# One layer of a hybrid decoder trunk on one core: reciprocal roots of the head norms moved from GpSimd to ScalarE and VectorE, a later and denser pace of head work, six part tiles in the down product, and a last block finished by halves

## The chip, the cores and the metric

The kernel runs on one core of one Trainium2 chip. The metric is the device time of one execution in microseconds (us), as the median of several runs. The engines are called by the names of the profile: PE is TensorE (matmuls), PEld its weight loads, DVE is VectorE, ACT is ScalarE, POOL is GpSimd, and SP is SyncE, whose queue issues nearly all of the kernel's DMA transfers, in the order of the program.

## The reference

One layer, 512 tokens, model width 2048, everything in float32:

```python
h = rms_norm(x, g)
p = h @ w_in                   # split: GLA q, k (512 each), v, r (1024 each), gate 16, attention q, k, v (1024 each)
A = gla_mixer(...)             # 4 heads, dk 128, dv 256; o = rms_norm(o) * silu(r) at its end
B = dilated_mixer(...)         # 8 heads of 128; q and k are normalised per head; three dilation patterns
x = x + concat(A, B) @ w_out
x = x + (silu(n @ w_gate) * (n @ w_up)) @ w_down     # n = rms_norm(x, g2), hidden width 5632
```

Two kinds of small norm matter here. Each head's q and k rows are divided by the root of their mean square over 128 columns, and each GLA output row by that over its 256 columns. The factor is (mean + eps)^(-1/2), one number per row and head.

## The kernel before

**The large products.** Every large product is done by one level of a scheme with seven products (in the order P1, P5, P6, P3, P7, P2, P4) in place of eight. The program names a piece of work a *pair*: two blocks of 512 output columns by 512 rows. There is one first pair with an order of its own, and 18 streamed ones: five for w_in (the last of them computes the gate r, "the gate pair"), two for w_out, eleven for the gate and up products of the feed-forward part, and six for w_down, which is the product "down": three thirds of the 5632 rows (i = 0, 1, 2) by two column halves (`np_` = 0, 1). A streamed pair has 28 items (21 in the last third of down). An item is one 128x1024 weight tile against an operand that is already in SBUF.

**One item.** float32 values are split in a high and a low part. For an item ACT casts the weight tile to the high part `wh` (L371), DVE subtracts to get the low part `wl` (L375), and PE does twelve 128x512 matmuls: eight with `wh`, four with `wl` (L398). `wh` and `wl` have two buffers each. Where an item's weight is a sum of two blocks, DVE forms that first (L296). The accumulators `acc` are two banks per product, for the two halves m = 0, 1 of its 256 rows; in every item the matmuls alternate between m = 0 and m = 1. When a product is done, DVE and ACT add its banks into `seed` tiles (L322, L334, L338), and `final` hands finished 128x512 blocks on.

**Work between the items.** After the eighth matmul of an item `p.step()` lets generators in the background do some units of their own: the eight attention heads, the GLA heads, the splitting of operands. How many units go into each item is set by a pace: for the gate pair `scripted(rate((27, 0.72), (1, 0)), GATE)` at L1219, which means 0.72 of a unit per item for 27 items, counted up, so that units fall on items 1, 2, 4, 5, 6, 8, 9, 11, 12, 13, 15 and so on. `hold=True` makes the sums of the pair wait behind the heads' instructions. Heads 4 to 7 become ready at the end of the pair ahead (columns 3584 and 4608, the q and k of these heads): its last blocks, called `cout`, are normalised by `heads_norm` and stored to a DRAM buffer `qb`, and the first unit of the heads (`dil_head`) loads from there the tiles q, qT, k and kT (L924 to L928), which PE transposes with an identity from `mats` (L935), ACT copies (L936), and from which PE makes scores (L944), DVE and ACT the softmax (L947 to L954), PE transposes again (L961) and multiplies with the values (L968). All instructions of an engine run in the order of the program; the heads' stand between those of the items.

**The norms' factor.** `rsqrt_mean` (L179 to L181) is called 24 times: 16 times in `heads_norm` on a tile `ss` of 128x4, and 8 times at L890 on a tile `so` of 128x2. It is two POOL instructions: multiply and add, then a power of -0.5 by a tensor `mhalf`. Ahead of it ACT has done Squares with sums (L1019 into `ss`, L889 into `so`); behind it DVE multiplies (L1021, L892) and SP stores (L1046).

**Operands of down.** The left operands of a third of down are fetched from DRAM in parts of 128x512 by `fetch_part` (L1148, DMA at L1152) into four tiles with the tags v, T, qT, kT in turn. ACT casts a part to the high half (L196), DVE subtracts the low half (L197) into the operand tiles `AA` and `AS`. `staged(items, 2)` (L1404) keeps the loads two parts ahead of the splitting. The parts of thirds 1 and 2 come during the second column half of the third ahead.

**Residual and end.** `final_down` (L1421) calls `residual` (L1229), which loads the earlier sum from `x1_d` or `y_d` into the tiles q and k (L1235) and adds it with DVE (L1237 where the accumulator is added in directly, L1240 where a `seed` tile is); the result is stored to `y_d` (L1433) or `out` (L1431). The last block of all is that of P4 in the last pair: two 128x512 halves that are added (L1237) and stored (L1431) when the last matmul is done.

## Time and profile before

| | |
|---|---|
| median of 3 runs | 1948.6 us (1947.58 to 1950.29) |
| profiled execution | 1952.11 us |
| its span, first to last instruction | 1950.0 us |
| mean granted TensorE clock | 0.998 |
| PE busy | 1916.9 us (98%), 9160 matmuls |
| DVE busy | 1647.6 us (84%) |
| ACT busy | 1088.9 us (56%) |
| POOL busy | 47.2 us (2%), 73 instructions |

The span begins with the first instruction and ends with the last one, so that 2.1 us of the profiled execution's time lie outside of it. A row of the timeline gives start, duration, engine, line, operation, output and inputs, and in square brackets how long the engine had been idle ahead of it and whose result ended that. A row of the windows gives a stretch of time, its length, the busy time of PE, PEld, DVE, ACT and POOL with the number of instructions, then the granted clock of PE, the share of the DMA engines and GB/s. SPq is the moment at which SP issues a transfer; the chain of waits has the time that the transfer itself takes.

### The profile page before, as it was taken

How to read it: one execution, taken by the hardware profiler on the slowest of the kernel's cores; microseconds unless marked ns; L12 is line 12 of the kernel's file. 1: busy time of each engine (PE TensorE's matmuls, PEld its weight loads, DVE VectorE, ACT ScalarE, POOL GpSimd, SP SyncE). 2: the span in 40 equal slices, each digit the busy share in tenths (PEclk: the TensorE clock that was granted, in tenths of full speed). 3: DMA queues.
4: the chain of work that ended last, by engine and by line, in shares of the span. 5: the costliest groups of instructions: out<-in, count | busy, mean ns of one | idle time of the engine just before them, and what ended most of it. 6: DMA issues, size and time to landing. Idle time of an engine off the chain costs nothing.

```text
span 1950.0 us, 25512 instructions
## 1 busy us (share of the span) xinstructions
PE 1916.9 (98%) x9160; PEld 1660.6 (85%) x9160; DVE 1647.6 (84%) x1845; ACT 1088.9 (56%) x1580; POOL 47.2 (2%) x73
## 2 busy tenths in 40 slices
PE   7999999999999999999999999999999999999998
PEld 6788888887888888888888888888888888888887
DVE  7996877767799999878878878878879989989987
ACT  8654564566676675544544544544546646546443
POOL 0000230001000000000000000000000000000000
PEclk9999999999999999999999999999999999999999
DMA  9445555454535563454464454453555765855662
GB/s 354 170 151 205 171 189 154 149 164 150 176 138 186 184 224 117 138 178 162 135 189 148 144 184 137 155 184 121 171 172 180 270 217 177 292 195 180 235 216 76
DMA packets 150791, 347.84 MB, mean 178 GB/s; under 512 B 15542, under 2 KB 42463, under 8 KB 150664
## 3 DMA queue, kind: packets, MB, share of 16 engines
q1 hardware_dynamic: 150520, 346.21, 53.5%
q8 instruction: 71, 1.16, 0.2%
q14 instruction: 56, 0.46, 0.1%
q10 hardware_dynamic: 144, 0.01, 0.0%
HBM read 288.20 MB, written 60.31 MB: 179 GB/s over the span
## 4 chain that ended last, share of the span: by engine, by line
PE 72%; DVE 7%; DMA 3%; issue 2%; ACT 1%; SPq 0%; POOLq 0%; POOL 0%; DVEq 0%; ACTq 0%
PE acc L398 68%; DVE wl L375 3%; PE bank L1059 1%; DVE wa L296 1%; PE bank L944 1%; PE bank L968 1%; DVE AS L197 1%; DMA wc<-in_w_in 0%; DMA p_d<-PT 0%; PE bank L935 0%; PE bank L961 0%; ACT wh L371 0%; DMA r<-p_d 0%; ACT jk L1019 0%; DMA q<-in_x 0%
## 5 line engine op out<-in xcount | busy, mean ns | idle before, releaser
L398 PE MATMUL acc<-wh,AS 128*128 128x512 f32 x3008 | 711.1, 379 | 0.0
L398 PEld LDWEIGHTS acc<-wh,AS 128*128 128x128 f32 x3008 | 568.6, 189 | 81.1 <-ACT wh L371 0.4
L371 ACT CAST wh<-wa 128x1024 fp32r<-128x1024 f32 x376 | 394.2, 1049 | 397.8 <-PE acc L398 357.7
L398 PE MATMUL acc<-wh,AA 128*128 128x512 f32 x2256 | 533.7, 379 | 2.8 <-ACT wh L371 2.8
L375 DVE TENSOR_TENSOR wl<-wa,wh 128x1024 fp32r<-128x1024 f32 x376 | 457.2, 1218 | 68.0 <-ACT wh L371 42.2
L398 PEld LDWEIGHTS acc<-wh,AA 128*128 128x128 f32 x2256 | 426.0, 189 | 64.5 <-ACT wh L371 4.0
L398 PE MATMUL acc<-wl,AS 128*128 128x512 f32 x1504 | 396.3, 385 | 3.9 <-DVE wl L375 3.8
L398 PEld LDWEIGHTS acc<-wl,AS 128*128 128x128 f32 x1504 | 280.1, 189 | 55.4 <-DVE wl L375 13.6
L398 PE MATMUL acc<-wl,AA 128*128 128x512 f32 x1128 | 295.1, 384 | 0.0
L398 PEld LDWEIGHTS acc<-wl,AA 128*128 128x128 f32 x1128 | 210.0, 189 | 29.8 <-issue 1.0
L371 ACT CAST wh<-wb 128x1024 fp32r<-128x1024 f32 x94 | 98.5, 1048 | 124.0 <-PE acc L398 118.4
L371 ACT CAST wh<-wc 128x1024 fp32r<-128x1024 f32 x94 | 98.5, 1047 | 110.8 <-PE acc L398 106.5
L371 ACT CAST wh<-wd 128x1024 fp32r<-128x1024 f32 x94 | 98.6, 1049 | 101.9 <-PE acc L398 93.3
L375 DVE TENSOR_TENSOR wl<-wc,wh 128x1024 fp32r<-128x1024 f32 x94 | 114.6, 1220 | 41.0 <-ACT wh L371 41.0
L375 DVE TENSOR_TENSOR wl<-wd,wh 128x1024 fp32r<-128x1024 f32 x94 | 114.4, 1219 | 38.9 <-ACT wh L371 30.1
L296 DVE TENSOR_TENSOR wa<-wc,wa 128x1024 f32<-128x1024 f32 x94 | 114.4, 1220 | 34.0 <-DMA wc<-in_w_gate 20.6
L375 DVE TENSOR_TENSOR wl<-wb,wh 128x1024 fp32r<-128x1024 f32 x94 | 114.1, 1217 | 4.8 <-ACT wh L371 4.5
L296 DVE TENSOR_TENSOR wa<-wb,wa 128x1024 f32<-128x1024 f32 x94 | 113.6, 1219 | 1.1 <-DMA wb<-in_w_in 0.4
L296 DVE TENSOR_TENSOR wb<-wd,wb 128x1024 f32<-128x1024 f32 x94 | 114.1, 1217 | 0.4
L296 DVE TENSOR_TENSOR wa<-wd,wa 128x1024 f32<-128x1024 f32 x94 | 113.0, 1217 | 0.8 <-DMA wd<-in_w_in 0.8
L338 DVE SCALAR_TENSOR_TENSOR seed<-acc,rs,seed 128x512 f32<-128x512 f32 x96 | 70.3, 745 | 27.8 <-PE acc L398 27.8
L322 ACT ACTIVATE seed<-acc,rs 128x512 f32<-128x512 f32 x96 | 60.7, 683 | 4.1 <-PE acc L398 4.1
(301 smaller groups left out, 1323.7 us busy)
## 6 DMA issues: line engine op xcount, KB each, us to landing
wa<-in_w_gate SPq DMA_DIRECT2D x44, 512.0 KB, 3.4
wb<-in_w_up SPq DMA_DIRECT2D x44, 512.0 KB, 4.4
wd<-in_w_up SPq DMA_DIRECT2D x44, 512.0 KB, 4.2
wc<-in_w_gate SPq DMA_DIRECT2D x44, 512.0 KB, 3.5
wc<-in_w_in SPq DMA_DIRECT2D x28, 512.0 KB, 3.5
wa<-in_w_in SPq DMA_DIRECT2D x24, 512.0 KB, 4.8
wb<-in_w_in SPq DMA_DIRECT2D x24, 512.0 KB, 5.9
wd<-in_w_in SPq DMA_DIRECT2D x24, 512.0 KB, 5.6
```

The lines of the kernel that those rows point to most:

```text
L197: nc.vector.tensor_tensor(a[:, :, 1, :], src, a[:, :, 0, :].bitcast(F32), op=ALU.subtract)
L296: nc.vector.tensor_tensor(src, other, src, op=ALU.subtract)
L322: nc.scalar.activation(halves(t), unfolded(src[m]), AF.Copy, scale=self.scale(half, m))
L338: nc.vector.scalar_tensor_tensor(halves(seed[m]), unfolded(src[m]), self.scale(half, m), halves(seed[m]), op0=ALU.mult, op1=ALU.add,)
L371: nc.scalar.copy(high[k], sources[k])
L375: nc.vector.tensor_tensor(low[k], sources.pop(k), high[k].bitcast(F32), op=ALU.subtract)
L398: nc.tensor.matmul(p.dst[prod][m], a[:, jj, hl, m * P : (m + 1) * P], folded(w[:, jj, :]), start=fresh and g == 0 and len(terms) == 2 and ...
L944: nc.tensor.matmul(lp[:, :n], qh[:, b * P : (b + 1) * P], kh[:, :n], start=True, stop=True)
L968: nc.tensor.matmul(op, vh[:, k, :], lgs[b][:, k * P : (k + 1) * P], start=(k == 0), stop=(k == b))
L1059: nc.tensor.transpose(bk[:, jj, m * P : (m + 1) * P], tiles[m][:, f : f + P], ident)
```

## The change

There are four parts.

1. `rsqrt_mean` no longer uses POOL. DVE multiplies and adds (L178 in the changed kernel), ACT takes the logarithm and the exponential of -0.5 times it (L179, L180) into a tile `rt` with four buffers, and DVE improves the root by one Newton step in three instructions (L181 to L183). Per call that is two POOL instructions less, four DVE and two ACT instructions more; the fill of `mhalf` is gone.
2. The gate pair's pace is 0 for three items, then 1, 0, 1, and 0.9 from there on. Units of the heads fall on items 3, 5, 7, 8, 9, 10, 11, 12, 13, 14, 15, 17, 18, 19, 20, 21 and so on.
3. The parts of thirds 1 and 2 of down go through six tiles (the tags oT and PT are added), four parts ahead of the splitting.
4. The very last item does its six matmuls for m = 0 first (four with `wh`, two with `wl`) and then the six for m = 1. The last block's residual is loaded into two `L` tiles; DVE adds m = 0 in one 128x512 instruction and m = 1 in two of 128x256; the first half of m = 1 is stored from ACT's queue, the rest from SP's.

```diff
-    mhalf = const([P, 8], "mhalf")
-    nc.gpsimd.memset(mhalf, -0.5)
-
-    def rsqrt_mean(dst, src, n):
-        nc.gpsimd.tensor_scalar(dst, src, 1.0 / n, EPS, op0=ALU.mult, op1=ALU.add)
-        nc.gpsimd.tensor_tensor(dst, dst, mhalf[:, : dst.shape[-1]], op=ALU.pow)
+    def rsqrt_mean(sq, n):
+        y = work("rt", (P, 4), bufs=4)[:, : sq.shape[-1]]
+        nc.vector.tensor_scalar(sq, sq, 1.0 / n, EPS, op0=ALU.mult, op1=ALU.add)
+        nc.scalar.activation(y, sq, AF.Ln)
+        nc.scalar.activation(y, y, AF.Exp, scale=-0.5)
+        nc.vector.scalar_tensor_tensor(sq, sq, -0.5, y, op0=ALU.mult, op1=ALU.mult)
+        nc.vector.tensor_tensor(sq, sq, y, op=ALU.mult)
+        nc.vector.scalar_tensor_tensor(sq, sq, 1.5, y, op0=ALU.add, op1=ALU.mult)
...
-            for w, terms in ((high.pop(k), (0, 1)), (low.pop(k), (0,))):
-                for jj in range(2):
-                    for m in range(2):
-                        for hl in terms:
...
+            order = [(i, m, jj, hl) for i in range(2) for jj in range(2) for m in range(2)
+                     for hl in range(2 - i)]
+            if k == last:
+                order.sort(key=lambda o: o[1])
+            for n, (i, m, jj, hl) in enumerate(order):
...
-    def fetch_part(src, half):
+    def fetch_part(src, half, tags=tags):
         def fetch():
-            t = work(tags[count[0] % 4], (P, 2, 256))
+            t = work(tags[count[0] % len(tags)], (P, 2, 256))
...
-    pair(opx, rows_in, col(2048), col(2560), final_gate, scripted(rate((27, 0.72), (1, 0)), GATE), row_scale, hold=True)
+    pair(opx, rows_in, col(2048), col(2560), final_gate, scripted(rate((3, 0), (1, 1), (1, 0), (1, 1), (1, 0.9)), GATE), row_scale, hold=True)
...
+    wide = tags + ("oT", "PT")
...
-                    (*fetch_part(*src), lambda t, name=name, g=g: op.split(name, g, t))
+                    (*fetch_part(*src, tags if i == 0 else wide), lambda t, name=name, g=g: op.split(name, g, t))
...
-        return staged(items, 2)
+        return staged(items, 2 if i == 0 else 4)
...
+            if i == 2 and np_ == 1 and tiles is None:
+                rs = [work("L", bufs=2) for _ in range(2)]
+                for m in range(2):
+                    load(rs[m], prev[rows[m]][:, c0 : c0 + 512])
+                for m in range(2):
+                    for b in range(1 if m == 0 else 2):
+                        c = slice(256 * b, 512 if m == 0 else 256 * b + 256)
+                        src, r = unfolded(acc_[m]), halves(rs[m])
+                        if m == 1:
+                            src, r = src[:, b], r[:, b]
+                        nc.vector.tensor_tensor(r, src, r, op=ALU.add)
+                        (nc.scalar.dma_start if m == 1 and b == 0 else store)(
+                            out[rows[m] * P : (rows[m] + 1) * P, c0 + c.start : c0 + c.stop],
+                            rs[m][:, c],
+                        )
+                return
```

The change also moves instructions on the engines. The first place is PE's order at the start of the gate pair, where heads 4 to 7 begin: `mats` is the identity, q, k, qT and kT are the tiles loaded for head 4, and `AS_69`, `AS_74` and `AS_81` are the operands of the pair's items 4, 5 and 6. Before:

```order
L398 MATMUL acc_4281<-wh_4261,AS_69_473 128x512 x2
L398 MATMUL acc_4280<-wh_4261,AS_69_473 128x512 x2
L398 MATMUL acc_4281<-wh_4261,AS_69_473 128x512 x2
L398 MATMUL acc_4280<-wl_4266,AS_69_473 128x512
L935 MATMUL bank_4233<-mats,q_4198 128x128 x4
L935 MATMUL bank_4239<-mats,k_4199 128x128 x4
L935 MATMUL bank_4245<-mats,qT_4206 128x128 x4
L935 MATMUL bank_4251<-mats,kT_4207 128x128 x4
L398 MATMUL acc_4281<-wl_4266,AS_69_473 128x512
```

And in the changed kernel, on the same engine (L402 and L939 are the old L398 and L935):

```order
L402 MATMUL acc_4375<-wh_4376,AS_74_505 128x512 x2
L402 MATMUL acc_4374<-wl_4381,AS_74_505 128x512
L402 MATMUL acc_4375<-wl_4381,AS_74_505 128x512
L402 MATMUL acc_4374<-wl_4381,AS_74_505 128x512
L402 MATMUL acc_4375<-wl_4381,AS_74_505 128x512
L402 MATMUL acc_4374<-wh_4397,AS_81_550 128x512
L939 MATMUL bank_4414<-mats,q_4354 128x128 x4
L939 MATMUL bank_4420<-mats,k_4355 128x128 x4
L939 MATMUL bank_4426<-mats,qT_4362 128x128 x4
L939 MATMUL bank_4432<-mats,kT_4363 128x128 x4
L402 MATMUL acc_4374<-wh_4397,AS_81_550 128x512
```

The transposes stood behind the ninth matmul of item 4 and now stand behind the first matmul of item 6. Between the two places lie the three other `wl` matmuls of item 4, the twelve of item 5 and one of item 6: sixteen matmuls.

The second place is DVE's order just ahead of that, where the two `cout` blocks that the heads load are normalised (`ss` holds the factors, `rt` the root of part 1, and L1183 prepares an operand for w_out). Before, from the multiply of the first block to the `wl` of item 4:

```order
L1021 TENSOR_TENSOR cout_4156<-cout_4156,ss_4160 128x512
L296 TENSOR_TENSOR wa_4144<-wb_4284,wa_4144 128x1024
L375 TENSOR_TENSOR wl_4223<-wa_4186,wh_4218 128x1024
L1021 TENSOR_TENSOR cout_4158<-cout_4158,ss_4170 128x512
L1183 TENSOR_TENSOR top_4522<-top_4522 128x512
L375 TENSOR_TENSOR wl_4266<-wa_4106,wh_4261 128x1024
```

And in the changed kernel, from the multiply of the first block to the `wl` of item 5, with the old L296, L375, L1021 and L1183 at L298, L377, L1025 and L1187:

```order
L1025 TENSOR_TENSOR cout_4264<-cout_4264,ss_4268 128x512
L178 TENSOR_SCALAR ss_4283<-ss_4283 128x4
L377 TENSOR_TENSOR wl_4325<-wa_4304,wh_4320 128x1024
L181 SCALAR_TENSOR_TENSOR ss_4283<-ss_4283,rt_4289 128x4
L1187 TENSOR_TENSOR top_4586<-top_4586 128x512
L182 TENSOR_TENSOR ss_4283<-ss_4283,rt_4289 128x4
L377 TENSOR_TENSOR wl_4344<-wa_4214,wh_4339 128x1024
L183 SCALAR_TENSOR_TENSOR ss_4283<-ss_4283,rt_4289 128x4
L298 TENSOR_TENSOR wa_4304<-wb_4399,wa_4304 128x1024
L1025 TENSOR_TENSOR cout_4266<-cout_4266,ss_4283 128x512
L377 TENSOR_TENSOR wl_4381<-wa_4232,wh_4376 128x1024
```

The second block's multiply stood directly behind the `wl` of item 3. Now the four small instructions of its factor are spread out, and the `wl` of item 4 and a sum of weights stand ahead of the multiply too. On ACT, each pair of L179 and L180 stands among the Squares, ahead of the next casts.

The third place is SP's queue in the first third of down, where the parts of the second third are loaded (L1152, in the changed kernel L1156) between stores of finished blocks (L1433, now L1454), loads of residuals (L1235, now L1239) and weight loads (L257, now L259). Before:

```order
L1433 DMA y_d_223<-seed_14002 128x512
L1235 DMA q_14198<-x_d_142 128x512
L1235 DMA k_14201<-x_d_143 128x512
L1152 DMA kT_14250<-S_d_209 128x512
L1152 DMA v_14273<-p_d_165 128x512
L1152 DMA T_14304<-p_d_167 128x512
L1152 DMA qT_14327<-p_d_169 128x512
L257 DMA wa_14394<-in_w_down 128x1024
```

And in the changed kernel:

```order
L1454 DMA y_d_221<-seed_14124 128x512
L1239 DMA q_14320<-x_d_140 128x512
L1239 DMA k_14323<-x_d_141 128x512
L1156 DMA T_14372<-p_d_165 128x512
L1156 DMA qT_14395<-p_d_167 128x512
L1156 DMA kT_14426<-p_d_169 128x512
L1156 DMA oT_14449<-p_d_163 128x512
L259 DMA wa_14516<-in_w_down 128x1024
```

Behind the same residual loads the first part that is loaded is now two parts further along in the list: those that stood there before have been issued ahead of the stores. At the very end of the program the two loads of the last block's residual (L1435) stand some forty entries of SP's queue ahead of the last store; before they (L1235) were the two entries directly ahead of the last two stores.

More of the change, by code (lines that the diff above doesn't have):

```diff
@@ L393, in stream @@
             fresh = prod in ("P1", "P5", "P2")
[L394 to L404 removed]
+            w = high.pop(k), low.pop(k)
+            order = [(i, m, jj, hl) for i in range(2) for jj in range(2) for m in range(2)
[3 more added lines that the diff above has]
+            for n, (i, m, jj, hl) in enumerate(order):
+                nc.tensor.matmul(
+                    p.dst[prod][m], a[:, jj, hl, m * P : (m + 1) * P], folded(w[i][:, jj, :]),
+                    start=fresh and g == 0 and i == 0 and jj == 0 and hl == 0,
+                    stop=g == p.op.groups - 1 and i == 1 and jj == 1,
+                    skip_group_check=not fresh,
+                )
+                if n == 7:
                     p.step()
@@ L889, in outputs @@
                 nc.scalar.activation(o[:, i, :], op[:, i, :], AF.Square, accum_out=so[:, i : i + 1])
-            rsqrt_mean(so, so, DV)
+            rsqrt_mean(so, DV)
             for i, t in enumerate(ts):
@@ L1019, in heads_norm @@
             nc.scalar.activation(jk, tv[:, h, :], AF.Square, accum_out=ss[:, h : h + 1])
-        rsqrt_mean(ss, ss, P)
+        rsqrt_mean(ss, P)
         nc.vector.tensor_tensor(
```

8 lines of the change are left out of this document (1 added, 7 removed).

## The prediction

> **What bounds the kernel now.** I read the page first: the span and the busy times.
>
> ```profile
> span 1950.0 us, 25512 instructions
> PE 1916.9 (98%) x9160; PEld 1660.6 (85%) x9160; DVE 1647.6 (84%) x1845; ACT 1088.9 (56%) x1580; POOL 47.2 (2%) x73
> ```
>
> PE is busy for 1916.9 of 1950.0 us, and the change takes no matmul away. So it can win only where PE stands still or runs with a lowered clock, at most 33 us plus what the clock costs. The second view is the waits of PE, summed by line and releaser (total us, times, longest).
>
> ```profile
> PE acc L398 <- DVE wl L375: 3.8, 8, 0.8
> PE bank L935 <- DMA q<-qb: 3.5, 1, 3.5
> PE acc L398 <- ACT wh L371: 2.8, 3, 1.3
> ...
> PE bank L961 <- DVE L L954: 0.8, 1, 0.8
> ```
>
> Of the stretch that the change touches, the first three rows are nearly all (the fourth is a wait inside a head); larger waits lie in the first pair, which stays as it is. The third view is the windows: start and end, length, busy time of PE, PEld, DVE, ACT, POOL, then the clock.
>
> ```profile
> 20.00:40.00 20.00, 16.72 (x74) 13.31 (x73) 17.70 (x20) 18.75 (x36) 2.93 (x4) 1.00 1.00 365
> 280.00:300.00 20.00, 19.27 (x104) 16.11 (x105) 18.82 (x22) 10.67 (x23) 6.47 (x6) 1.00 0.19 62
> 460.00:480.00 20.00, 16.49 (x79) 13.94 (x78) 12.69 (x23) 12.09 (x27) 3.88 (x4) 0.91 0.30 102
> 500.00:520.00 20.00, 20.00 (x111) 17.65 (x109) 9.32 (x16) 11.70 (x19) 0.00 (x0) 1.00 0.53 169
> 560.00:580.00 20.00, 19.44 (x96) 16.19 (x95) 20.00 (x26) 17.19 (x27) 0.00 (x0) 1.00 0.26 98
> 1660.00:1680.00 20.00, 18.75 (x87) 15.83 (x86) 19.38 (x25) 10.09 (x13) 0.00 (x0) 1.00 0.90 288
> 1800.00:1820.00 20.00, 18.88 (x88) 15.86 (x87) 19.51 (x24) 10.28 (x14) 0.00 (x0) 1.00 0.91 313
> ```
>
> The change can win in three places: 460 to 480 us (gate heads), 1660 to 1680 and 1800 to 1820 (down), and the end. PE's clock is 0.91 only in the first, so 20 x 0.09 = 1.8 us go there beside the wait of 3.5. Elsewhere PE is dense, and beside it DVE is often full: 20.00 of 20 from 560 us.
>
> **Term 1, later gate heads: -1.9 us.** Here is the start of the heads on the timeline.
>
> ```profile
> 461.96 0.19 ACT L1019 ACTIVATION_READ_ACCUMULATOR jk<-cout 128x1 f32 x1
> 463.21 1.86 POOL L181 TENSOR_TENSOR ss<-ss,mhalf 128x4 f32<-128x4 f32 x1
> 465.11 0.69 DVE L1021 TENSOR_TENSOR cout<-cout,ss 128x512 f32<-128x512 f32 x1 [0.90 <-POOL ss L181]
> 467.69 0.38 PE L398 MATMUL acc<-wl,AS 128*128 128x512 f32 x1
> 471.54 0.66 PE L935 MATMUL bank<-mats,q 128*128 128x128 f32 x4 [3.47 <-DMA q<-qb]
> ```
>
> And two pieces of the chain of waits there, with start and length:
>
> ```profile
> 465.83 2.03 DMA qb<-cout
> ...
> 467.92 3.58 DMA q<-qb
> ```
>
> The second block's multiply ends at 465.80, its store takes 2.03, the load of q 3.58, and PE, which has arrived at 468.07, starts the transposes at 471.54.
>
> In the changed order sixteen matmuls more lie ahead of the transposes. A dense stretch of the chain of waits gives the price of one, 52.10 / 240 = 0.217:
>
> ```profile
> 961.52 52.10 PE acc L398 x240
> ```
>
> So PE arrives at 468.07 + 16 x 0.217 = 471.5. But the load comes later too. Between the Squares and the second multiply now lie on DVE the four small instructions, a `wl` more, a sum of weights and an operand's step (all in the order). Placing them one behind the other by their durations (1.22 for `wl` and for a sum of the same shape, 0.69 for the step and for the multiply, 0.15 for each small one, by rows here and below), behind the Squares' end at 462.15 and the first block's multiply, which the same line-up ends at 462.7, I get: L178 at 462.8, `wl` to 464.2, L181 and L1187 to 465.1, L182 and the next `wl` to 466.5, L183, the sum to 467.85, the multiply to 468.55. That is 2.75 us later than 465.80. With 2.03 and 3.58 and the gaps between them, q lands at about 474.3. PE waits some 2.8 us in place of 3.47, and 0.65 us is won.
>
> The clock is the larger part. An idle time of 2.40 us ahead of one matmul left the clock at 1.00 (window 20 to 40 us); the one of 3.47 took it to 0.91.
>
> ```profile
> 33.50 0.70 PE L461 MATMUL acc<-wh,AS 128*128 128x512 f32 x2 [2.40 <-DVE AS L209]
> ```
>
> The new wait of about 2.8 lies between the two, nearer to the one that was free. I take the clock as kept: -1.8. Against it stands the denser pace. From item 7 on every item carries a unit, in place of 0.72, so the heads' chains have fewer matmuls between them to cover their latencies. The trace's wait inside a head, 0.8 us, is the nearest row; I take most of one more such wait, +0.6. Sum -0.65 - 1.8 + 0.6 = -1.9. Ends: both wait and clock loss gone, -5.3; wait as long as before, clock still falling and the units costing 2 us, +2. DVE's 9.32 of 20 us at 500 speaks for room there.
>
> [...] No run here shows a wait between 2.4 and 3.47.
>
> **Term 2, six tiles for the down parts: -2.2 us.** Where the first third's second half meets the loads of the next third, ACT stands in front of a part that hasn't come, and its cast of the next weight tile is queued behind it.
>
> ```profile
> 1664.71 0.73 PEld L398 LDWEIGHTS acc<-wl,AS 128*128 128x128 f32 x4 [0.23 <-DVE wl L375]
> ...
> 1670.70 0.62 ACT L196 CAST AS<-kT 128x512 fp32r<-128x512 f32 x1 [4.72 <-DMA kT<-S_d]
> 1672.30 1.23 DVE L375 TENSOR_TENSOR wl<-wc,wh 128x1024 fp32r<-128x1024 f32 x1 [0.62 <-ACT wh L371]
> 1672.32 1.99 PE L398 MATMUL acc<-wh,AA 128*128 128x512 f32 x8 [1.25 <-ACT wh L371]
> ...
> 1819.01 1.99 PE L398 MATMUL acc<-wh,AA 128*128 128x512 f32 x8 [1.12 <-ACT wh L371]
> ```
>
> The chain of waits has the load itself:
>
> ```profile
> 1664.88 5.74 DMA kT<-S_d
> ```
>
> With four tiles the load of kT is issued behind the residual's q and k, at 1664.88, and takes 5.74 us. With six tiles and a lead of four parts, the part that stood there has been issued two parts earlier, ahead of the stores and residual loads that hold SP's queue (the order's third place). Two parts are about two items, 5 us, more than the 4.72 that ACT waited. Both waits go: 1.25 + 1.12 = 2.37. Next late is DVE, 19.38 and 19.51 of 20 us busy in these windows; PE's weight load had to wait 0.23 for a `wl` at 1664.71 already. I leave 0.2 for it: -2.2. Ends: 0 if DVE's queue takes over at once, -2.8 with the small waits on `wl`.
>
> **Term 3, the end by halves: -1.3 us.**
>
> ```profile
> 1943.59 1.03 PE L398 MATMUL acc<-wl,AA 128*128 128x512 f32 x4
> 1945.07 0.69 DVE L1237 TENSOR_TENSOR q<-acc,q 128x512 f32<-128x512 f32 x1 [3.64 <-DMA q<-y_d]
> 1945.80 0.69 DVE L1237 TENSOR_TENSOR k<-acc,k 128x512 f32<-128x512 f32 x1
> 1946.52 0.34 SPq L1431 DMA_DIRECT2D out<-k  x1
> ```
>
> PE ends at 1944.62, two additions follow, the second ending at 1946.49, then the store, and the span ends at 1950.0, 3.5 us behind the issue. Now m = 0 is complete six matmuls, 1.3 us, ahead of PE's end, and its residual was loaded long before, so its addition runs under the last matmuls. Behind PE's end come two additions of half size, about 0.4 each with their gaps: done at 1945.45, in place of 1946.49, 1.05 earlier. Half as large a last store may land some 0.2 sooner. Ends: 0, if the first of the two stores, issued by ACT, is slower to land by as much; -2.5, if the stores land with their size.
>
> **Term 4, norms without POOL: +0.6 us.** Here are the removed instructions on the 128x4 factors and a multiply behind them (count, total us, mean ns, then idle time and what ended it), and behind these, from the instructions of one tile, two small ones as they are added, in another norm of the kernel (ns):
>
> ```profile
> L180 POOL TENSOR_SCALAR ss<-ss 128x4 f32<-128x4 f32 x16 | 7.3, 455 | 156.8 <-ACT jk L1019 156.7
> L181 POOL TENSOR_TENSOR ss<-ss,mhalf 128x4 f32<-128x4 f32 x16 | 17.8, 1115 | 1.3
> L1021 DVE TENSOR_TENSOR seed<-seed,ss 128x512 f32<-128x512 f32 x12 | 8.3, 692 | 16.0 <-POOL ss L181 14.2 <-ACT wh L371 1.7
> ```
>
> ```profile
> L1316 ACT ACTIVATE rt<-ms x1: 212/212/212, 729.1 to 729.1; 128x4 f32<-128x4 f32 x1
> L1319 DVE SCALAR_TENSOR_TENSOR ms<-ms,rt x1: 152/152/152, 731.6 to 731.6; 128x4 f32<-128x4 f32 x1
> ```
>
> DVE gets 24 x 4 x 0.155 = 15 us, ACT 24 x 2 x 0.21 = 10 us, and POOL, which nobody else needs, loses its part. A chain of 4 x 0.155 + 2 x 0.21 = 1.04 us stands against POOL's 1.57, so alone it would be quicker; but it crosses between two busy engines twice and stands in line on each. Before, DVE sat idle for POOL 14.2 us ahead of 12 of these multiplies, while PE's whole wait for `wl` was 3.8 us. What hides the new 15 us is the same idle time: DVE is busy 18.82 of 20 in the worst of the windows with norms. Where that cover is thin PE waits for `wl` (8 times, 3.8 us now). I take one or two tenths for a handful of calls, and half the idle time won back: +0.6. Ends: -0.5 and +4 (0.16 us for each call, one more small instruction ahead of a `wl` that was just in time).
>
> **Sum.** -1.9 - 2.2 - 1.3 + 0.6 = -4.8. The span becomes 1945.2 and the profiled time 1947.3 from 1952.1. The runs' median lies 3.5 below the profiled time, so 1943.8.
>
> **Rivals.**
>
> A. Every wait goes. If ACT and DVE place the norm's steps sooner than my line-up, by 2.8 us, q is there when PE arrives: term 1 is -5.3 with no cost of density, the sum -8.2, the time 1940.4. For it: PE's sixteen matmuls are 3.45 us, as long as the wait was. Against it: the order puts a `wl` and a sum ahead of the multiply. Chance 0.2.
>
> B. The gate heads win nothing: the change puts the heads later, but the load moves as far, PE waits 3.4 us again, the clock falls, and the dense pace meets the full DVE (20.00 of 20 from 560 us) an item or two earlier. Term 1 is +1, the sum -1.9, the time 1946.7. For it: the multiply's delay of 2.75 has eaten most of 3.45 already, and 0.6 more would bring the wait to the old length. Chance 0.26.
>
> C. Slower: the norms' factors in line on DVE. L181 stands behind L178 on DVE, and must wait until ACT has done Ln and Exp; if ACT is in a weight cast (1049 ns by the row below), DVE stands still for it, and the `wl` queued behind is late for PE. At 24 calls this would be 0.5 us each, 12 us, +12 - 5.4 = +6.6, the time 1955.2. It decides from 9.3 us, 0.39 per call: then the other terms' 5.4 are lost and 3.9 more. For it: DVE already ends some `wl` only when PE asks. Against it: the scheduler has put other work between L178 and L181 in the order of the second block, and DVE's present waits for POOL cost PE next to nothing (term 4). Chance 0.12.
>
> ```profile
> L371 ACT CAST wh<-wa 128x1024 fp32r<-128x1024 f32 x376 | 394.2, 1049 | 397.8 <-PE acc L398 357.7
> ```
>
> The forecast itself: 0.42.
>
> **Range and chances.** A measurement of this kernel tells some 0.2%, 3.9 us, from no change: faster is under 1944.7, slower over 1952.5. The forecast's own range is 1942 to 1946, two thirds of it faster; A is faster, B within, C slower. Faster 0.28 + 0.2 + a little of B, 0.5; slower 0.12; within, the rest. For 8 in 10 the range goes from 1939 (A with its ends) to 1949 (B, with term 4 at +3).
>
> **What would show it.** In the changed profile: (1) ahead of the first transposes at L939 a wait of about 2.8 us for q<-qb, and a clock of 1.00 in that window; a clock of 0.9 would make term 1 wrong by 1.8. (2) No wait of ACT for a part near 1670 and 1817, none of PE for `wh` over 0.3. (3) DVE's last addition at 0.8 us behind PE's end, the span's end some 4.3 behind it in place of 5.4. (4) L1025's idle time without POOL, and PE's total wait for `wl` below 5 us; over 10 would be rival C.

## The result, and the profile after

| | before | changed |
|---|---|---|
| median of 7 runs each | 1950.29 us (1946.55 to 1953.17) | 1943.59 us (1939.34 to 1945.43) |
| ratio, 95% interval | | 0.9958 [0.9947, 0.9969], that is -8.2 us (-10.3 to -6.0) |
| profiled execution, span | 1952.11, 1950.0 us | 1939.89, 1938.0 us |

The time is 0.2 us from the forecast of 1943.8, but so close a hit is luck. Over more runs the kernel before has a median of 1950.29, not 1948.6, and the gain is larger than the forecast 4.8 by about as much: 6.7 us between the two medians, 8.2 by the ratio, and the interval holds both. The two profiled executions differ by 12.0 us, more than the medians. They have to be compared stage by stage, since an execution also has gains and losses of 0.5 to 2 us that fall at random; falls of the clock, told in the last section, are a large part of them.

Here are the span and busy times of the changed kernel's page.

```profile
span 1938.0 us, 25589 instructions
PE 1913.2 (99%) x9160; PEld 1660.0 (86%) x9160; DVE 1657.8 (86%) x1942; ACT 1093.7 (56%) x1628; POOL 10.6 (1%) x24
```

DVE has 10 us more to do, ACT 5, POOL 37 less; PE stands still for 25 us in place of 33. PE's waits, by line and releaser (L402 is the old L398, L939 the old L935, L1063 the old L1059):

```profile
PE bank L1063 <- DVE seed L1108: 1.6, 2, 1.3
...
PE acc L402 <- DVE wl L377: 1.4, 5, 0.4
...
PE bank L939 <- DMA q<-qb: 0.9, 1, 0.9
```

The wait for the heads' load fell from 3.5 to 0.9, that for `wl` from 3.8 to 1.4, and the row with ACT's `wh` of a streamed item is gone. New is a wait of 1.3 at L1063. The windows at the three places:

```profile
460.00:480.00 20.00, 18.91 (x98) 16.24 (x97) 18.00 (x31) 14.16 (x26) 0.00 (x0) 1.00 0.24 78
...
1660.00:1680.00 20.00, 19.92 (x93) 17.02 (x92) 20.00 (x26) 11.62 (x16) 0.00 (x0) 1.00 0.98 347
1800.00:1820.00 20.00, 19.92 (x92) 16.86 (x91) 19.47 (x25) 9.40 (x11) 0.00 (x0) 1.00 0.94 318
```

The clock stays at 1.00 at the heads' start, and in down PE is busy for 19.92 of 20 us where it was 18.75 and 18.88, while DVE is as full as it was.

**Stage by stage.** In every kernel here the 24 streamed pairs (5 + 2 + 11 + 6; the 18 named at the start are those ahead of down) have the same 7896 matmuls, in the same order but for the inside of the very last item. So the start of the first matmul of an item can be set against that of the same item in the kernel before. The table has the change in each stretch of items in us, one profiled execution each. Items 112 to 139 are the gate pair, 532 to 615 most of the first two thirds of down.

| items | changed | norms only | pace only | tiles only | end only | all but norms | all but pace |
|---|---|---|---|---|---|---|---|
| 56 to 84 | -2.0 | -1.3 | -0.5 | +0.2 | +0.6 | +0.7 | -1.7 |
| 112 to 140 | -3.5 | -4.4 | -3.6 | -0.3 | -0.4 | -2.3 | -4.5 |
| 532 to 616 | -3.0 | -0.9 | +1.2 | -3.1 | -1.7 | -3.0 | -3.0 |
| last item to the end | -1.5 | +0.2 | +1.0 | +0.5 | -1.5 | -1.5 | -1.5 |
| all others | -1.9 | -0.3 | -1.1 | -0.2 | +0.2 | -0.1 | -2.0 |
| span | -12.0 | -6.6 | -3.0 | -2.9 | -2.9 | -6.2 | -12.7 |

The row of all others, in which the parts hardly act, shows the size of chance: from +0.2 to -2.0, although most of these kernels share the same instructions there. Two entries hold a fall of the clock: that of "all but norms" in the gate pair, behind its wait at 139.8 (a clock of 0.91 in the window 560 to 580), and that of "pace only" in 532 to 616 (0.91 from 1660 to 1680). Each is worth some 1.7 us, an estimate from the 3.41 us at a clock of 0.50 that the last section shows. And the profiled execution before has 1.1 us of small waits between items 537 and 545 that no other trace has, so that every entry in the row 532 to 616 is that much too low. Where a part acts, the single waits tell more. This second table has the time from the start of one matmul to that of the next (0.22 when dense) at the places that stand out; item 57.12 is the twelfth matmul of item 57. At 61.8 and 139.8 matmuls of other work lie between, so that their dense values are higher.

| place | POOL norms (5 traces) | norms on DVE and ACT (8 traces, with Newton) |
|---|---|---|
| 57.12 | 0.42 to 0.84 | 0.21 to 0.22 |
| 61.8 | 1.76 to 1.99 | 1.01 |

| place | without the part | with the part |
|---|---|---|
| 553.12, six tiles | 1.52 to 2.53 (5) | 0.21 to 0.22 (9) |
| 609.12, six tiles | 0.91 to 1.50 (5) | 0.21 to 0.22 (9) |
| 139.8, the change's pace | 1.51 to 1.90 (5) | 2.35 to 3.17 (6) |

### The profile page after: what moved, and what is told of

It reads as the page before. It is cut to its first block, busy times and chain, and to the rows that moved or that the text cites. A ratio compares the mean times of both kernels' runs of the same rounds, so it can differ in the third digit from the quotient of the medians.

```text
span 1938.0 us, 25589 instructions
## 1 busy us (share of the span) xinstructions
PE 1913.2 (99%) x9160; PEld 1660.0 (86%) x9160; DVE 1657.8 (86%) x1942; ACT 1093.7 (56%) x1628; POOL 10.6 (1%) x24
## 4 chain that ended last, share of the span: by engine, by line
PE 84%; DVE 9%; DMA 3%; issue 3%; ACT 1%; SPq 0%; DVEq 0%; ACTq 0%
PE acc L402 78%; DVE wl L377 3%; PE bank L1063 1%; DVE wa L298 1%; PE bank L972 1%; DVE wl L517 1%; PE bank L948 1%; DVE AS L199 1%; PE bank L965 0%; DVE AS L211 0%; PE acc L465 0%; DMA wc<-in_w_in 0%; DMA wa<-in_w_in 0%; DMA wb<-in_w_in 0%; PE bank L887 0%
## 5 line engine op out<-in xcount | busy, mean ns | idle before, releaser
L402 PE MATMUL acc<-wh,AS 128*128 128x512 f32 x3008 | 711.4, 379 | 0.0
L402 PEld LDWEIGHTS acc<-wh,AS 128*128 128x128 f32 x3008 | 568.3, 189 | 80.7 <-ACT wh L373 0.3
L402 PE MATMUL acc<-wh,AA 128*128 128x512 f32 x2256 | 533.5, 379 | 0.0
L377 DVE TENSOR_TENSOR wl<-wa,wh 128x1024 fp32r<-128x1024 f32 x376 | 457.8, 1220 | 70.8 <-ACT wh L373 45.3
L402 PEld LDWEIGHTS acc<-wh,AA 128*128 128x128 f32 x2256 | 426.3, 189 | 60.5
L402 PE MATMUL acc<-wl,AS 128*128 128x512 f32 x1504 | 394.0, 384 | 1.6 <-DVE wl L377 1.4
L402 PEld LDWEIGHTS acc<-wl,AS 128*128 128x128 f32 x1504 | 280.1, 189 | 51.0 <-DVE wl L377 9.2
L402 PE MATMUL acc<-wl,AA 128*128 128x512 f32 x1128 | 295.6, 384 | 0.2
L402 PEld LDWEIGHTS acc<-wl,AA 128*128 128x128 f32 x1128 | 209.7, 189 | 30.9 <-DVE wl L377 2.0
L377 DVE TENSOR_TENSOR wl<-wc,wh 128x1024 fp32r<-128x1024 f32 x94 | 114.7, 1221 | 41.4 <-ACT wh L373 41.3
L377 DVE TENSOR_TENSOR wl<-wd,wh 128x1024 fp32r<-128x1024 f32 x94 | 114.6, 1221 | 36.3 <-ACT wh L373 29.4
L298 DVE TENSOR_TENSOR wa<-wc,wa 128x1024 f32<-128x1024 f32 x94 | 114.5, 1222 | 31.4 <-DMA wc<-in_w_gate 19.8
L377 DVE TENSOR_TENSOR wl<-wb,wh 128x1024 fp32r<-128x1024 f32 x94 | 114.2, 1218 | 4.7 <-ACT wh L373 4.5
L298 DVE TENSOR_TENSOR wa<-wb,wa 128x1024 f32<-128x1024 f32 x94 | 113.8, 1220 | 1.6 <-DMA wb<-in_w_in 0.9
L298 DVE TENSOR_TENSOR wb<-wd,wb 128x1024 f32<-128x1024 f32 x94 | 114.2, 1220 | 0.4
L298 DVE TENSOR_TENSOR wa<-wd,wa 128x1024 f32<-128x1024 f32 x94 | 113.3, 1220 | 0.1
```

What stands on the lines that cost most here:

```text
L298: nc.vector.tensor_tensor(src, other, src, op=ALU.subtract)
L377: nc.vector.tensor_tensor(low[k], sources.pop(k), high[k].bitcast(F32), op=ALU.subtract)
L402: nc.tensor.matmul(p.dst[prod][m], a[:, jj, hl, m * P : (m + 1) * P], folded(w[i][:, jj, :]), start=fresh and g == 0 and i == 0 and jj == ...
```

## The experiments

Each kernel is an edit of the kernel before or of the changed one. A ratio is against the kernel before, run beside it on the same chip, from 5 to 12 executions of the edited kernel. Of the diffs, the lines that tell the edit are shown; of the line with the pace, only the pace.

**Norms only** (part 1 of the diff on the kernel before):

```diff
-        nc.gpsimd.tensor_scalar(dst, src, 1.0 / n, EPS, op0=ALU.mult, op1=ALU.add)
-        nc.gpsimd.tensor_tensor(dst, dst, mhalf[:, : dst.shape[-1]], op=ALU.pow)
...
+        nc.vector.tensor_scalar(sq, sq, 1.0 / n, EPS, op0=ALU.mult, op1=ALU.add)
+        nc.scalar.activation(y, sq, AF.Ln)
...
```

> Part 1 alone on the kernel before (norm factors on DVE and ACT, old pace, old tiles, old end). By the prediction's term 4 it costs 0.6 us (-0.5 to +4), and the heads' start keeps its wait of about 3.5 us with the clock at 0.91. The theory read from the two traces: it wins some 2.0 us in three waits of PE between 270 and 335 us, and the order alone already puts the heads' transposes 14 matmuls later (place 1415 among the streamed matmuls, before 1401, in the full change 1417), so that the wait is about 1.4 us, the clock stays at 1.00, and some 3.5 us more are won: -5.5 in all.

Measured 0.9968 [0.9956, 0.998], -6.2 us; stages -1.3 and -4.4. In this kernel the heads' start reads as follows (L937 is the old L935):

```profile
464.57 0.68 DVE L1023 TENSOR_TENSOR cout<-cout,ss 128x512 f32<-128x512 f32 x1
...
467.40 0.37 SPq L926 DMA_DIRECT2D q<-qb  x1
...
470.41 0.66 PE L937 MATMUL bank<-mats,q 128*128 128x128 f32 x4 [0.95 <-DMA q<-qb]
```

The pace is the old one, and yet PE waits only 0.95 us, with a clock of 1.00:

```profile
460.00:480.00 20.00, 18.96 (x97) 15.48 (x95) 15.62 (x39) 13.76 (x32) 0.00 (x0) 1.00 0.24 79
```

Term 4's cost of 0.6 falls; the second theory's -5.5 lies in the interval. Part 1 alone does what the prediction put down to the pace.

**Pace only** (part 2 on the kernel before):

```diff
-scripted(rate((27, 0.72), (1, 0)), GATE)
+scripted(rate((3, 0), (1, 1), (1, 0), (1, 1), (1, 0.9)), GATE)
```

> Part 2 alone (the pace of the gate pair, POOL norms). The order puts the transposes 11 matmuls later than before. By the prediction's rule the load is then not later at all, so PE waits 3.47 - 11 x 0.217 = 1.1 us, the clock stays at 1.00, and with 0.6 to 0.7 of density: -3.4 us. The rival that density or DVE eats it (B) expects 0 or above and a clock that still falls.

Measured 0.999 [0.9981, 0.9998], -2.0 us; the stage of the gate pair -3.6. The wait for the load is gone but for 0.2, and the clock there stays at 1.00:

```profile
460.00:480.00 20.00, 19.50 (x99) 16.66 (x98) 17.71 (x23) 14.23 (x27) 4.25 (x4) 1.00 0.33 106
```

So the pace by itself wins at the heads' start. The span's remainder is chance, the largest piece a clock that fell in down (0.91 in the window 1660 to 1680; last section).

**Tiles only** (part 3) and **end only** (part 4), each on the kernel before, as in the diff of the change:

```diff
+    wide = tags + ("oT", "PT")
...
-        return staged(items, 2)
+        return staged(items, 2 if i == 0 else 4)
```

> Part 3 alone (six tiles, four parts ahead). By the prediction -2.2 us, at 1670 and 1817 us, and nothing anywhere else. By the two traces -2.7: also 0.5 of small waits near 1643. The rival that DVE takes over expects less than 1.

```diff
+            if k == last:
+                order.sort(key=lambda o: o[1])
...
```

> Part 4 alone (last item by halves, early loads, three additions, two queues). By the prediction -1.3 us, by the two traces -1.5, all of it behind the start of the last item; nothing before it moves. The rival that the end is set by how long a last store takes to land expects 0.

Measured 0.9986 [0.9978, 0.9995], -2.7 us, and 0.9993 [0.9983, 1.0002], -1.4 us. The two waits in down are gone in the first and there in the second; the end is 1.5 us shorter in the second and not in the first. The interval of the second includes no change at all; what shows its gain is the last item, 1.45 to 1.48 us shorter than before in all eight traces that have part 4 whole. Behind each removed wait PE now waits 0.24 for `wl` and 0.10 at the matmul behind it: DVE is the next one late.

**All but norms** and **all but pace** (the change with one part undone, by the reverse of the first two diffs):

```diff
...
-        nc.scalar.activation(y, sq, AF.Ln)
...
+        nc.gpsimd.tensor_tensor(dst, dst, mhalf[:, : dst.shape[-1]], op=ALU.pow)
```

> The full change without part 1 (POOL norms stay). If the parts add up and part 1 cost 0.6 us, this is 0.6 faster than the full change. If part 1 wins 2.0 between 270 and 335 us and the pace alone keeps the clock, it is 2 us slower than the full change: about -7 to -8 against the kernel before in a profile. At the heads' start PE should wait about 1.1 us.

```diff
-scripted(rate((3, 0), (1, 1), (1, 0), (1, 1), (1, 0.9)), GATE)
+scripted(rate((27, 0.72), (1, 0)), GATE)
```

> The full change without part 2 (old pace). By the prediction (the later pace is what wins at the heads' start) this loses 1.9 us against the full change. If the order's own move by part 1 is enough, the transposes stand at place 1415 in place of 1417, PE waits some 1.4 us with the clock at 1.00, the less dense pace costs less, and the time is the same as the full change within 1 us, or lower.

Measured 0.9958 [0.9945, 0.997] and 0.9949 [0.9937, 0.9962]. The times cannot tell either from the full change (0.9958). The stages can: without part 1, items 56 to 84 take 2.7 us more than with it, 1.4 of it at the two places of the table; the rest is at 73.8, which varies in all kernels. Without part 2, the gate pair takes 1.0 us less: four traces with both parts have it 3.4 to 4.0 us shorter than before, the two with part 1 alone 4.4 and 4.5. So part 2 on top of part 1 is a small loss in this stretch. Where it loses is the new wait, here in the changed kernel, with its cause on DVE and SP:

```profile
545.36 0.33 SPq L259 DMA_DIRECT2D wd<-in_w_out  x1
545.74 0.90 SPq L1088 DMA_DIRECT2D og<-ong_d  x2
...
551.84 1.34 DVE L1104 TENSOR_TENSOR og<-seed,og 128x512 f32<-128x512 f32 x2 [1.72 <-DMA og<-ong_d]
...
556.19 0.33 PE L1063 MATMUL bank<-mats,seed 128*128 128x128 f32 x1 [1.31 <-DVE seed L1108]
```

And with the old pace:

```profile
544.67 1.09 SPq L1088 DMA_DIRECT2D og<-ong_d  x2
...
550.11 1.42 DVE L1104 TENSOR_TENSOR og<-seed,og 128x512 f32<-128x512 f32 x2
```

With the change's pace a weight load `wd` of 512 KB has slipped ahead of the load of the GLA outputs `og` in SP's queue; og lands later, DVE waits 1.72, and PE at the end of that chain 1.31. All six traces with that pace have the two loads in this order, `og` issued 8.8 us ahead of the matmul at 139.8 in place of 9.7, and the longer wait there (in the table); none of the five with the old pace has either. That it is the queue's order and not the traffic was read from these rows, not tried by itself.

**No Newton** (the change without its three correcting instructions on DVE; the factor is then the exponential itself):

```diff
-        nc.scalar.activation(y, y, AF.Exp, scale=-0.5)
-        nc.vector.scalar_tensor_tensor(sq, sq, -0.5, y, op0=ALU.mult, op1=ALU.mult)
-        nc.vector.tensor_tensor(sq, sq, y, op=ALU.mult)
-        nc.vector.scalar_tensor_tensor(sq, sq, 1.5, y, op0=ALU.add, op1=ALU.mult)
+        nc.scalar.activation(sq, y, AF.Exp, scale=-0.5)
```

> The full change without the three Newton instructions on DVE (the factor is the exponential itself; 72 DVE instructions fewer). If DVE's added work in line costs anything (rival C, or a part of term 4), this is faster than the full change, by up to 0.16 us per call, 4 us. If the cover holds, the difference is under 0.5 us in the stretch between 270 and 335 us, and the heads' load is sooner by some 0.5 us.

Measured 0.9944 [0.993, 0.9957], which the times can't tell from the full change. In items 56 to 84 it is 1.9 us slower, not faster: instructions stand in other places there, with waits of 0.4 at 57.12 and 58.12, and a longer one at 73.8, which varies in all kernels (0.22 to 1.86). The heads' wait is 0.2, but a wait of 0.8 inside the head follows. So 72 DVE instructions, 11 us of work, cost nothing that shows. Rival C falls.

**One item later still**, **thinner**, and **later and thinner** (the change with other paces):

```diff
-rate((3, 0), (1, 1), (1, 0), (1, 1), (1, 0.9))
+rate((4, 0), (1, 1), (1, 0), (1, 1), (1, 0.9))
```

> The full change with the heads one item later still (pace 0 for four items). The transposes then stand 7 matmuls, 1.5 us, later, so the wait of 0.9 us is gone. If nothing is given back this wins 0.9 us. If the heads' units, being later, push work into the stretch from 540 us where DVE is full, it is equal or slower.

```diff
+rate((3, 0), (1, 1), (1, 0), (1, 1), (1, 0.72))
```

> The full change, heads begun as late (units at items 3, 5, ...) but then at the old 0.72 of a unit per item. If the density from item 7 on is what costs the 1.3 us wait of PE for a seed tile of the gate's sums (139th item, 3.0 us there in place of 1.6), that wait is gone and the stretch of items 112 to 140 is 1.0 to 1.4 us shorter than with the full change, as with the old pace. If the late start causes it, it stays.

```diff
+rate((4, 0), (1, 1), (1, 0), (1, 1), (1, 0.8))
```

> The full change with the heads another item later and then 0.8 of a unit per item: no wait for the heads' load (as in the run one item later) and no dense end. If both savings add, the stretch of items 112 to 140 is some 1.5 us shorter than with the full change and no longer than with the old pace; if the heads' work is only pushed to the end of the pair, a wait of 1 us or more comes back there.

Measured 0.9938 [0.9925, 0.995], 0.9967 [0.9956, 0.9978] and 0.9966 [0.9954, 0.9978]. The first has no wait for the load and only 0.2 at L1063, but one of 1.1 for `wh`; its gate pair is 1.5 us shorter than the changed kernel's and it has the lowest ratio here, though its interval overlaps that of the change. The other two do end the wait at 139.8, as expected, but win nothing by it. In the thinner one PE waits 2.9 us inside a head, in the pair, and the pair is 1.0 us longer than the changed kernel's, not shorter. In the later and thinner one the pair is 1.5 us shorter, although PE waits 1.8 at L1063 in it. But the work that is left falls behind the pair, PE waits another 2.6 at L1063 there, and behind that wait the clock falls (0.91 in the window 560 to 580, by the same estimate some 1.7 us more):

```profile
PE bank L1063 <- DVE cr L1108: 2.6, 1, 2.6
...
PE bank L1063 <- DVE seed L1108: 1.8, 1, 1.8
```

Items 112 to 168 are 0.9 and 0.5 us shorter than before, the changed kernel's 3.5. So in these runs a lower density did not pay; where each unit falls decides.

**Two edits undone in stretches apart**, twice, with one profiled execution of each kernel, so that only single places can be read (their times are 1942.98 and 1943.7 us). First a lead of two with six tiles, and the old order in the last item; then four tiles with a lead of four, and the old ending with the new order:

```diff
-        return staged(items, 2 if i == 0 else 4)
+        return staged(items, 2)
...
-            if k == last:
-                order.sort(key=lambda o: o[1])
```

> The full change with two edits undone, which act in stretches apart. Six tiles, but a lead of two parts as before: if the tiles matter and not the lead, the two waits in down (items 553 and 609) stay gone; if the lead matters, 1.4 and 1.3 us come back. And the last item in its old order, with the early loads and the addition in three pieces kept: if the order matters, the end is 0.5 to 0.7 us later than with the full change (a whole 128x512 addition more behind PE's end); if only the early load matters, the same.

```diff
-    wide = tags + ("oT", "PT")
+    wide = tags
...
-            if i == 2 and np_ == 1 and tiles is None:
-                rs = [work("L", bufs=2) for _ in range(2)]
...
```

> The full change with two other edits undone. Four tiles with a lead of four parts: the order then has the loads where they stood before, so both waits in down should be back, 1.4 and 1.3 us; if the lead alone were enough they stay gone. And the last item ordered by halves, but with the old ending (residual loaded late, two whole additions, SP's queue alone): the additions wait for the residual until some 0.3 us behind PE's end, so the end is as before, about 1.5 to 1.9 us later than with the full change; if the order alone wins, it keeps half of it.

With six tiles and the old lead both waits stay gone (0.21 and 0.22). With four tiles and the longer lead they are back (2.53 and 1.02). It is the tiles, not the lead. At the end, the early loads without the order, with the addition in three pieces and the two queues kept, are 0.84 us later than all together; the order without the early loads is 2.1 us later, as late as the old end. In that kernel the additions wait for the residual as before:

```profile
1935.33 0.59 PE L402 MATMUL acc<-wl,AA 128*128 128x512 f32 x2
1937.05 0.69 DVE L1241 TENSOR_TENSOR q<-acc,q 128x512 f32<-128x512 f32 x1 [4.31 <-DMA q<-y_d]
```

PE ended at 1935.92; the first addition began 1.13 later. So the order pays only with the new ending, and the new ending pays without the order. What of it is the early load, the pieces or the second queue was not separated.

## Why the prediction was right, and where it was wrong

**The time** was right, by two errors that cancel: the kernel before is 1.7 us slower than the median the forecast began from, and the gain, 6.7 us between the medians, is 1.9 more than the forecast 4.8 (by the ratio it is 8.2, from 6.0 to 10.3). Two terms held, two did not.

**Term 2, the tiles** (-2.2): held. The two places took 2.08 and 1.13 us on the mean of five traces and 0.22 with the part, a gain of 2.8, of which 0.34 is given back to DVE behind each: -2.1. The next one late was DVE, as forecast. ACT's wait for a part, 4.72 us, is down to this one row:

```profile
1662.67 0.62 ACT L198 CAST AA<-T 128x512 fp32r<-128x512 f32 x1 [0.26 <-DMA T<-p_d]
```

**Term 3, the end** (-1.3): held, a little low: -1.5 against the profiled execution before, -1.9 against the mean of the five traces with the old ending. The rows are those that were forecast:

```profile
1932.88 0.69 DVE L1442 TENSOR_TENSOR L<-acc,L 128x512 f32<-128x512 f32 x1 [1.93 <-PE acc L402]
1933.54 0.59 PE L402 MATMUL acc<-wl,AA 128*128 128x512 f32 x2
...
1934.18 0.76 DVE L1442 TENSOR_TENSOR L<-acc,L 128x256 f32<-128x256 f32 x2 [0.60 <-PE acc L402]
```

The last addition ends 0.8 behind PE's end, as said, 1.07 sooner than before (1.05 was said); the span ends 3.9 behind it, where 4.3 was said. The 0.2 for a smaller last store had no row to stand on; from the end of the last addition to the end of the span it is now 3.1 us where it was 3.5, so that the store came 0.4 sooner. Whether its size did that no run shows.

**Term 4, the norms** (+0.6): wrong in its sign. The failed step is that DVE's idle time for POOL was called free because PE's whole wait for `wl` was small. But two of PE's few waits hung on the norms. At the first, in the kernel before, DVE stands still for POOL ahead of a multiply, and the multiply of the GLA output (L892) is the next in its order:

```profile
271.24 0.69 DVE L1021 TENSOR_TENSOR seed<-seed,ss 128x512 f32<-128x512 f32 x1 [2.23 <-POOL ss L181]
...
276.08 0.38 ACT L889 ACTIVATE oT<-bank 128x256 f32<-128x256 f32 x1 [3.00 <-DMA ong_d<-oT]
...
280.22 1.99 PE L398 MATMUL acc<-wh,AA 128*128 128x512 f32 x8 [0.46 <-ACT wh L371]
```

and the row of ACT in the changed one:

```profile
275.33 0.38 ACT L893 ACTIVATE oT<-bank 128x256 f32<-128x256 f32 x1 [2.35 <-DMA ong_d<-oT]
```

The factor comes sooner, so the store of the GLA output is issued 0.54 us sooner against item 57, and ACT waits 0.65 less for its tile. ACT's order has changed too: one pair of Squares and sums (L1019) stands ahead of the `wh` cast where three stood, which brings the cast 0.71 us nearer to the tile. Together the cast ends 1.2 us sooner on the means of the five traces and the eight. The order is enough by itself where six tiles have the old lead: the tile came no sooner than with the pace alone (1.22 and 1.35 us ahead of item 57), and PE did not wait. The earlier store alone is not to be counted on: without Newton it was issued first of all, yet ACT waited 3.12 us for the tile and PE lost 0.4 at 57.12. The other, 61.8, is one of order alone. Before, three sums of weights stood in a row ahead of a `wl`:

```profile
288.46 1.22 DVE L296 TENSOR_TENSOR wb<-wd,wb 128x1024 f32<-128x1024 f32 x1
289.60 1.21 DVE L296 TENSOR_TENSOR wa<-wd,wa 128x1024 f32<-128x1024 f32 x1
290.73 1.21 DVE L296 TENSOR_TENSOR wb<-wd,wb 128x1024 f32<-128x1024 f32 x1
291.87 1.21 DVE L375 TENSOR_TENSOR wl<-wa,wh 128x1024 fp32r<-128x1024 f32 x1
```

With the norms' small instructions in the list, the `wl` has come ahead of the last of the three:

```profile
287.71 1.21 DVE L298 TENSOR_TENSOR wb<-wd,wb 128x1024 f32<-128x1024 f32 x1
288.85 0.68 DVE L1025 TENSOR_TENSOR cout<-cout,ss 128x512 f32<-128x512 f32 x1
289.45 1.21 DVE L377 TENSOR_TENSOR wl<-wa,wh 128x1024 fp32r<-128x1024 f32 x1
290.58 1.22 DVE L298 TENSOR_TENSOR wb<-wd,wb 128x1024 f32<-128x1024 f32 x1
```

The places 57.12 and 61.8 are worth 0.46 and 0.85 us on the means, 1.3 in all. Why the order came out so was not tried.

**Term 1, the gate heads** (-1.9): the mechanism at the place was right (a shorter wait, and a clock that is kept). Its size, -3.5 in the stage, and its owner were not as forecast. The steps that were off are two. The line-up put the second block's multiply 2.75 us later; with the 2.1 us by which the changed kernel is ahead at item 112 added, it ends 1.6 later. The nine instructions of that line began 0.4 us sooner than placed, and each began 0.08 to 0.10 before the end of the one ahead, 0.7 in all. And the load took 2.83 in place of 3.58 us; why was not tried. So PE waits 0.94 us, not 2.8 (3.47 + 1.6 - 0.75 - 3.45 is 0.9). These are the rows of the multiply and of PE, and behind them the store and the load in the chain of waits:

```profile
464.61 0.69 DVE L1025 TENSOR_TENSOR cout<-cout,ss 128x512 f32<-128x512 f32 x1
...
469.02 0.38 PE L402 MATMUL acc<-wh,AS 128*128 128x512 f32 x1
...
470.33 0.66 PE L939 MATMUL bank<-mats,q 128*128 128x128 f32 x4 [0.94 <-DMA q<-qb]
```

```profile
465.36 2.03 DMA qb<-cout
...
467.45 2.83 DMA q<-qb
```

The owner: I gave all of it to the pace. The place of the transposes among the streamed matmuls was 1401; with the norms alone it is 1415, with the pace alone 1412, with both 1417. Either part is enough to keep the clock there (1.00 in the window 460 to 480 with each) and to remove most of the wait (0.95 and 0.2 us are left), so their gains of 4.4 and 3.6 don't add up, and the pace's own new wait is what remains of it: 1.3 us in one place, where the term had 0.6 for density.

**The clock.** I set 2.8 us between a wait that kept the clock (2.40) and one that lost it (3.47). No run put the heads' wait between them. But the two marks could not tell: elsewhere one wait of 2.15 us lost the clock, another of 2.15 and one of 2.9 kept it (last section). Divided at the steps of 3.4133 us that are told there, the 2.40 has pieces of 1.26 and 1.14 us, the 3.47 of 1.20 and 2.27. Whether a wait of 2.8 us at this place would have kept the clock, no run shows. So the step to "kept" was right only because the wait came out at 0.94.

**Rivals.** A asked for a load in time; it was 0.9 us off, and the sum of gains came near to A's 8.2 by other ways. B is ruled out by the changed kernel itself, with 0.94 us and a clock of 1.00; of its dense pace that meets DVE there is the wait of 1.3 at 139.8. C did not show in any run.

## What to carry to other kernels

A change of which engine does a small step also moves other instructions in the order: read from the order what each part alone moves before crediting a gain to the part that was meant for it. Call an engine's idle time free only after following what is released behind it (here a store, a tile, a cast), not by the bottleneck's total wait. And compare two traces item by item: where the single waits have the same size in every trace of one kind and never in the other, they settle what a span with 2 us of chance cannot.

## What the runs showed of the hardware that was not expected

The same wait of PE at the same place did and did not cost the clock. In the kernel with the pace alone and in the one with four tiles, PE waits 2.15 us for `wh` in down, and the eight matmuls behind it take 2.66 us in the first and 1.99 in the second:

```profile
1666.98 2.66 PE L398 MATMUL acc<-wh,AA 128*128 128x512 f32 x8 [2.15 <-ACT wh L371]
```

```profile
1663.34 1.99 PE L402 MATMUL acc<-wh,AA 128*128 128x512 f32 x8 [2.15 <-ACT wh L373]
```

The record of the granted clock in the traces tells the two apart. In the kernel before it begins at 11.89 us into the span and shows two falls to 0.50: at 472.69 us, for 3.41 us, and at 1947.24, behind PE's end. They lie 135 and 567 steps of 3.4133 us behind the record's start. In the changed kernel it begins at 12.41 us, and its one fall, at 1937.53, behind PE's end, is 564 such steps later. Here are three steps of the kernel before at the heads' start, with the wait of 3.47 us in the first two:

```profile
465.86:469.27 3.41, 2.21 (x11) 1.59 (x9) 3.41 (x5) 3.10 (x5) 0.00 (x0) 1.00 0.25 90
469.27:472.68 3.41, 1.14 (x10) 1.14 (x11) 1.21 (x2) 0.45 (x1) 0.00 (x0) 1.00 0.49 143
472.68:476.10 3.42, 3.42 (x15) 3.04 (x14) 0.43 (x3) 2.77 (x7) 0.00 (x0) 0.50 0.00 0
```

PE is idle for 1.20 us of the first and 2.27 us of the second, and the third has half the clock. With the pace alone, the whole wait of 2.15 us lies in the 3.41 us ahead of the fall at 1668.17 us:

```profile
1664.76:1668.17 3.41, 1.26 (x7) 1.05 (x6) 1.89 (x4) 2.80 (x4) 0.00 (x0) 1.00 0.97 384
1668.17:1671.58 3.41, 3.41 (x10) 2.68 (x9) 3.41 (x6) 1.99 (x4) 0.00 (x0) 0.50 0.63 165
```

With four tiles, the wait lies across two such stretches, PE is idle for 1.5 and 0.6 us of them, and the clock stays:

```profile
1659.30:1662.71 3.41, 1.89 (x9) 1.21 (x7) 2.50 (x4) 0.98 (x2) 0.00 (x0) 1.00 1.00 374
1662.71:1666.12 3.41, 2.78 (x13) 2.46 (x14) 2.80 (x4) 3.31 (x5) 0.00 (x0) 1.00 0.60 240
```

In the kernel with the thinner pace even a wait of 2.9 us, which lies across two with 1.3 and 1.6 us idle, left the clock at 1.00:

```profile
PE bank L948 <- ACT k L940: 2.9, 1, 2.9
```

```profile
515.94:519.35 3.41, 2.09 (x10) 1.50 (x8) 2.23 (x3) 2.41 (x5) 0.00 (x0) 1.00 0.67 264
519.35:522.76 3.41, 1.85 (x10) 1.58 (x11) 1.93 (x6) 3.41 (x8) 0.00 (x0) 1.00 0.88 288
522.76:526.18 3.42, 3.42 (x22) 2.85 (x21) 3.12 (x10) 3.42 (x10) 0.00 (x0) 1.00 0.08 25
```

In the changed kernel the clock stays at 1.00 from 12.41 us to PE's end. Of the steps up to there, the one with the most idle time of PE has 1.67 us of it (the first here):

```profile
29.48:32.89 3.41, 1.74 (x7) 0.94 (x5) 2.80 (x3) 3.41 (x8) 0.00 (x0) 1.00 1.05 410
32.89:36.31 3.42, 2.60 (x12) 2.31 (x13) 3.42 (x5) 3.42 (x8) 0.00 (x0) 1.00 1.02 406
```

In the kernel before, the most up to PE's end in a step behind which the clock stayed is 1.52 us, from 28.95. So the length of a whole wait doesn't tell in these traces which one cost the clock: 2.15 and 3.47 did, 2.15, 2.40 and 2.9 did not. In the rows above, the idle time in the 3.41 us ahead of a fall is 2.27 and 2.15 us, and 1.67 or less where the clock stayed. They give no limit: without part 1 PE is idle for 1.73 us of the whole window from 540 to 580, and yet the clock is 0.91 from 560 to 580. What made it fall there no run separated.

By the 0.50 and the 3.41 us, a fall where PE is dense costs 1.7 us, an estimate. By the clock's mean that is also most of the spread between executions: of the seven of the changed kernel, the two with a mean granted clock of 1.000 have spans of 1937.6 and 1938.0 us, the one with 0.997 has 1943.6, and 0.003 of that is 5.8 us. The mean over 54 executions of the kernel before is 0.9978, over the seven of the changed one 0.9986, over five with the norms alone 0.9988, over twelve with the pace alone 0.9982. A thousandth of the span is 1.9 us, so of the gain about 1.6 us, give or take 0.8, lie in the clock by estimate, near the 1.8 that term 1 had for it.
